# A decoder trunk on one core: a convolution tail joined on TensorE, a new order of the first blocks and of five normalizations

## The chip, the cores and the metric

The kernel runs on one core of one Trainium2 chip. A core has five engines with queues of their own: TensorE (PE; its weight loads are listed as PEld), VectorE (DVE), ScalarE (ACT), GpSimd (POOL) and SyncE (SP), which here only issues transfers. The metric is the device time of one execution in microseconds. Shown are the median of three runs and one profiled execution, from whose trace all rows come.

## The reference

One inference step of a two-layer decoder trunk, for 256 prompt tokens and 8 samples of one token, 264 columns in all, model width 2048, all in 32-bit floats. Layer 0 mixes tokens with a convolution module, layer 1 with an mLSTM; both have a gated feed-forward network and a gated addition of an embedding. The change lies in the convolution module and in the normalizations:

```python
def conformer_conv(x, past, w_in, b_in, w_dw, b_dw, ln_g, ln_b, w_out, b_out):
    a, gt = jnp.split(x @ w_in + b_in, 2, axis=-1)
    u = a * jax.nn.sigmoid(gt)
    y, new_past = causal_dwconv(u, past, w_dw, b_dw)      # 31 taps for each of 2048 channels
    y = jax.nn.silu(layer_norm(y, ln_g, ln_b))
    return y @ w_out + b_out, new_past

for i in range(DEPTH):                                    # 2 layers
    x = layer_norm(ALPHA * x + mixer(x), ln_mix_g[i], ln_mix_b[i])
    x = layer_norm(ALPHA * x + conv_ffn(x), ln_ffn_g[i], ln_ffn_b[i])
    x = x + sigmoid(x @ pl_w_gate[i]) * rms_norm(p[i] @ pl_w_proj[i], pl_g[i])
```

## The kernel before

Activations lie feature by feature: 16 chunks of 128 features (partitions) by 264 columns. A product of a weight matrix runs in blocks of output chunks. For each block the weights come from memory in raw tiles of 1 MB (512 KB where a block has one output chunk), and a half of such a tile is split: `whi` is its rounded copy (ACT, line 246), `wlo` the rest (DVE or POOL, line 247). Activations are split likewise into XH and XL, and a product is the sum of three fast ones, whi x XH, whi x XL and wlo x XH (lines 263 to 265; with LAG, lines 271, 272 and 277, the XL products one chunk later). Some halves are *native*: PE multiplies the raw 32-bit weights with X directly (line 236), for which no split is needed, and which the trace shows as two records a product.

The convolution's input product has ten blocks (`BLOCKS`). Block 0 is all native; X itself arrives during it, two chunks at a time (`load`, which `wblock` calls as a hook while it issues the weights' transfers), and is split for the later blocks. The parameter tile `par` is loaded when `load` is called with `PARK`, its second half in block 1, after which a small DVE operation on `par` follows. `NAT` says how many halves of each block are native, `VLO` how many low parts are DVE's instead of POOL's. After a block's product the gate gives U, and the 31 taps of the convolution follow for its chunk or two: `GT` taps as ACT products and POOL additions (in cscr, then joined to Y), `PT` taps on PE as products with diagonal matrices (`diags` makes these on ACT from the identity; `join_pe`), the rest on DVE. The last blocks' taps form a tail with little product work beside it.

Then comes the LayerNorm of the convolution (`ln` with silu=True). Its mean and mean square are PE products with a constant matrix (line 409): lne is a sum of two chunks of Y on DVE, lnq one of squares; between them stand `emb` products (line 516), the products p W_p of the embeddings, which are needed much later and fill PE here. The shift (a mean of the first chunks) is subtracted from chunks 12 to 15 on DVE at the end of the joins. After the reciprocal on DVE, a list of steps sets the order on DVE and ACT: `CVSEQ` here, `LNSEQ` in the four plain LayerNorms. A step is a letter, a chunk and a count: s subtracts the mean from chunks, m multiplies (and lets ACT write silu or XH), l forms XL, o copies an emb product, h marks from which half on the weights' casts come behind that point. The product with cv_w_out follows; its first four chunks are native (`WON`), with Y as operand.

`high_priority` and `after` (an order without a wait) shape the queues; within an engine, instructions run in the queue's order.

Of the kernel before, what the change touches and what calls it, by code (L numbers as in the profile page):

```python
# [12 lines left out]
F32 = mybir.dt.float32  # L13
# [26 lines left out]
GT = [4, 4, 3, 4, 4, 5, 6, 10, 9, 5]  # L40
# [5 lines left out]
VLO = {2: 3}  # L46
# [16 lines left out]
LNSEQ = ("m0:1 o0:1 m1:1 s2:2 m2:2 l0:1 o0:8 l1:1 s4:4 m4:4 l2:2 h8:0 s8:4 l4:2 m8:2 l6:1 m10:2 l7:1 l8:1 s12:4 "  # L63
         "m12:2 h14:0 l9:1 m14:2 l10:6")

CVSEQ = ("m0:1 h4:0 o0:1 m1:3 s4:4 l0:1 o0:8 l1:1 m4:4 l3:1 l2:1 s8:2 s10:1 m8:1 "
         "s11:1 l4:1 m9:1 l5:1 s13:1 s12:1 m11:1 l6:2 s14:2 m10:1 m15:1 l9:1 l8:1 m12:1 "
         "m13:2 l10:1 l11:1 l14:1 l15:1 l12:1 l13:1")
# [5 lines left out]
PARK = 8  # L74
# [4 lines left out]

XC = 4  # L80
# [10 lines left out]

BIG = 1e30
# [24 lines left out]
def _body(ctx, tc, nc, I, O):  # L117
# [52 lines left out]

    ident = const.tile([P, P], F32, name="ident")
    make_identity(nc, ident)
    ones = const.tile([P, P], F32, name="ones")
    g.memset(ones, 1.0)
# [4 lines left out]
    dummy = const.tile([P, 1], F32, name="dummy")  # L179
    mask = const.tile([P, P], F32, name="mask")  # L180
# [27 lines left out]
    wdma, wlast = [None], [None]  # L208


    def wblock(W, cols, rhs, nk, acc, k0=0, loe=None, hook=None, fine=False, native=None, hold=(), lag=0, stage=0, side=None, whole=None):
# [4 lines left out]
        for kg in range(0, nk, 2 * kq):  # L216
# [4 lines left out]
            for ka, step in ([(k, 2) for k in range(0, kn, 2)] if fine else [(0, kn)]):  # L221
# [3 lines left out]
                for c0, w in cols:  # L225
# [3 lines left out]
                    at += w  # L229
            for h0 in range(0, kn, kq):  # L230
                for f in (side or {}).get(kg + h0, ()):
                    f()
# [12 lines left out]
                with tc.high_priority(AHEAD):  # L245
                    whi = s.copy(hi[:, :, :width], r)  # L246
                    wlo = e.tensor_tensor(lo[:, :, :width], r, f32(hi[:, :, :width]), ALU.subtract)  # L247
                for k, first in hold:
# [110 lines left out]
    def ln(Y, gn, bn, off, outs, silu=False, acc=None, emb=(), pq=None, behind=None, steps=LNSEQ):  # L359
# [83 lines left out]
        if silu:  # L443
            sub(2, 2)
        dv(v.reciprocal(r, r))
        for op, c, n in _seq(steps):
# [10 lines left out]
    ln_state = None  # L457

# [84 lines left out]
    def conv_mixer():  # L543
# [16 lines left out]
        def diags():  # L560
# [12 lines left out]
        def load(k, n):  # L573
            dma.dma_start(X[:, k:k + n], I["xT"][:, k:k + n])
            if k == PARK:
                dma.dma_start(par[:, :NPC], I["par"][:, :NPC])
            for c in range(k, k + n):
                split(XH[:, c], XL[:, c], X[:, c])
# [3 lines left out]
        joins, tails, late, later, tapped, formed = [], [], [], [], [None], [None]  # L582
        for bi, (c0, n) in enumerate(blocks):
# [32 lines left out]
            with tc.high_priority(2 * AHEAD if last else GLU):  # L616
# [4 lines left out]
                for j in range(n):  # L621
# [4 lines left out]
                    s.copy(w, u)  # L626
# [591 lines left out]
```

## Time and profile before

| what | value |
|---|---|
| time, median of 3 runs | 2523.67 us (2522.7 to 2524.24) |
| profiled execution | 2524.14 us, span 2522.4 us |
| PE busy | 2504.5 us (99%) |
| DVE, ACT, POOL busy | 1613.7 (64%), 1256.9 (50%), 235.0 us (9%) |

The span is the time from the first to the last record of the profile; the execution's own time has some 1.7 us around it. The granted clock of TensorE is given as a share of full speed. In the timeline a row is a run of like instructions on one engine: its start, its length, what it is and how many, and in brackets the idle time ahead of it and what ended that.

### The profile page before, as it was taken

What the parts mean: (1) busy time and instruction counts of PE and PEld (TensorE: products, weight loads), DVE (VectorE), ACT (ScalarE), POOL (GpSimd) and SP (SyncE); (2) the same over time, 40 slices, a digit from 0 to 9 for tenths busy, and PEclk for the clock granted to TensorE, in tenths of its full rate; (3) what the DMA queues carried; (4) which work ended last, traced back from release to release, by engine and by line L of the source; (5) the groups of instructions that cost most, each with busy time, mean ns of one, the idle gap of its engine ahead of it and who ended that gap; (6) DMA issues with size and microseconds to landing.
All of it is one profiled execution on the core that took longest, in us unless ns stands there. A gap on an engine that the chain in (4) does not pass through costs nothing.

```text
span 2522.4 us, 47218 instructions
## 1 busy us (share of the span) xinstructions
PE 2504.5 (99%) x20000; PEld 2478.1 (98%) x20000; DVE 1613.7 (64%) x2429; ACT 1256.9 (50%) x1773; POOL 235.0 (9%) x203
## 2 busy tenths in 40 slices
PE   9999999999999999999999999999999999999999
PEld 8998999999999999999999999999999999999999
DVE  6898586555445555488678787775555445555586
ACT  6556464444334444346566666464444334444363
POOL 6985000000000000000010011000000000000000
PEclk9999999999999999999999999999999999999999
DMA  7646546555555556545687786555555555656553
GB/s 254 192 152 215 184 147 201 184 183 177 177 183 184 184 178 206 181 163 193 202 293 243 235 285 220 197 180 184 181 177 180 183 184 169 190 178 206 184 172 135
DMA packets 271110, 486.54 MB, mean 193 GB/s; under 512 B 12170, under 2 KB 72330, under 8 KB 270482
## 3 DMA queue, kind: packets, MB, share of 16 engines
q1 hardware_dynamic: 263410, 456.19, 55.9%
q0 software_dynamic: 7488, 27.33, 3.1%
q8 instruction: 156, 2.56, 0.4%
q14 instruction: 56, 0.46, 0.1%
HBM read 465.77 MB, written 19.68 MB: 192 GB/s over the span
## 4 chain that ended last, share of the span: by engine, by line
PE 89%; DVE 6%; issue 2%; DMA 1%; POOL 1%; ACT 1%; SPq 0%; POOLq 0%; DVEq 0%
PE acc L264 27%; PE acc L263 27%; PE acc L265 27%; PE acc L236 2%; DVE Y L149 2%; DVE X L149 1%; PE acc L277 1%; DVE X L146 1%; DVE wlo L247 1%; POOL cscr L146 1%; PE acc L271 1%; DVE XL L149 1%; PE acc L272 1%; DMA spare<-scr 0%; DMA raw<-in_cv_w_in 0%
## 5 line engine op out<-in xcount | busy, mean ns | idle before, releaser
L247 DVE TENSOR_TENSOR wlo<-raw,whi 128x1024 fp32r<-128x1024 f32 x749 | 916.9, 1227 | 731.4 <-ACT whi L246 730.0
L246 ACT CAST whi<-raw 128x1024 fp32r<-128x1024 f32 x794 | 828.8, 1048 | 1022.1 <-PE acc L264 965.4
L264 PE MATMUL acc<-XL,whi 128*128 128x264 f32 x3840 | 1088.1, 284 | 0.0
L263 PE MATMUL acc<-XH,whi 128*128 128x264 f32 x3840 | 1084.1, 285 | 0.4 <-ACT whi L246 0.3
L265 PE MATMUL acc<-XH,wlo 128*128 128x264 f32 x3840 | 1083.8, 284 | 0.4 <-POOL wlo L247 0.3
L264 PEld LDWEIGHTS acc<-XL,whi 128*128 128x128 f32 x3840 | 722.7, 188 | 0.5
L263 PEld LDWEIGHTS acc<-XH,whi 128*128 128x128 f32 x3840 | 720.5, 189 | 1.5 <-ACT whi L246 0.5
L265 PEld LDWEIGHTS acc<-XH,wlo 128*128 128x128 f32 x3840 | 719.0, 188 | 1.2 <-POOL wlo L247 1.0
L264 PE MATMUL acc<-ha,whi 128*128 128x264 f32 x1024 | 290.5, 284 | 0.0
L265 PE MATMUL acc<-ha,wlo 128*128 128x264 f32 x1024 | 290.3, 284 | 0.0
L263 PE MATMUL acc<-ha,whi 128*128 128x264 f32 x1024 | 288.8, 285 | 0.0
L247 POOL TENSOR_TENSOR wlo<-raw,whi 128x1024 fp32r<-128x1024 f32 x45 | 109.4, 2444 | 1724.8 <-ACT whi L246 1724.8
L263 PE MATMUL acc<-xo,whi 128*128 128x264 f32 x768 | 223.6, 291 | 0.0
L264 PE MATMUL acc<-xo,whi 128*128 128x264 f32 x768 | 220.6, 287 | 0.0
L265 PE MATMUL acc<-xo,wlo 128*128 128x264 f32 x768 | 219.9, 286 | 0.0
L264 PEld LDWEIGHTS acc<-ha,whi 128*128 128x128 f32 x1024 | 192.8, 188 | 0.1
L265 PEld LDWEIGHTS acc<-ha,wlo 128*128 128x128 f32 x1024 | 192.3, 188 | 0.0
L263 PEld LDWEIGHTS acc<-ha,whi 128*128 128x128 f32 x1024 | 192.0, 189 | 0.1
L263 PEld LDWEIGHTS acc<-xo,whi 128*128 128x128 f32 x768 | 144.8, 189 | 0.7
L264 PEld LDWEIGHTS acc<-xo,whi 128*128 128x128 f32 x768 | 144.7, 188 | 0.8
L265 PEld LDWEIGHTS acc<-xo,wlo 128*128 128x128 f32 x768 | 144.5, 188 | 0.3
L149 DVE SCALAR_TENSOR_TENSOR Y<-U,par,Y 128x227 f32<-128x227 f32 (+24 forms) x337 | 131.7, 452 | 13.1 <-ACT Y L627 8.2
(294 smaller groups left out, 2578.9 us busy)
## 6 DMA issues: line engine op xcount, KB each, us to landing
raw<-in_ff_w_gate SPq DMA_DIRECT2D x88, 1024.0 KB, 5.2
raw<-in_ff_w_up SPq DMA_DIRECT2D x88, 1024.0 KB, 5.1
raw<-in_ff_w_down SPq DMA_DIRECT2D x88, 1024.0 KB, 5.0
raw<-in_pl_w_gate SPq DMA_DIRECT2D x32, 1024.0 KB, 5.2
raw<-in_ml_w_in SPq DMA_DIRECT2D x32, 1024.0 KB, 6.6
raw<-in_cv_w_in SPq DMA_DIRECT2D x60, 512.0 KB, 5.9
raw<-in_cv_w_out SPq DMA_DIRECT2D x16, 1024.0 KB, 5.0
raw<-in_ml_w_in SPq DMA_DIRECT2D x32, 512.0 KB, 4.7
```

The lines of the kernel that those rows point to most:

```text
L146: return e.tensor_tensor(o, a, b, op)
L149: return v.scalar_tensor_tensor(o, a, sc, b, op0, op1)
L236: pe.matmul(acc[j], raw[:, kc - kg, j * P:(j + 1) * P], (whole or X)[:, kc], start=kc == 0, stop=kc == nk - 1)
L246: whi = s.copy(hi[:, :, :width], r)
L247: wlo = e.tensor_tensor(lo[:, :, :width], r, f32(hi[:, :, :width]), ALU.subtract)
L263: pe.matmul(acc[j], wh, xh, start=kc == 0, stop=False)
L264: pe.matmul(acc[j], wh, xl, start=False, stop=False)
L265: wlast[0] = pe.matmul(acc[j], wl, xh, start=False, stop=kc == nk - 1)
L271: pe.matmul(acc[j], hi[:, k2, j * P:(j + 1) * P], xh, start=kc == 0, stop=False)
L272: wlast[0] = pe.matmul(acc[j], lo[:, k2, j * P:(j + 1) * P], xh, start=False, stop=False)
L277: pe.matmul(acc[j], whs[j], xl, start=False, stop=k0_ == nk - 1)
```

## The change

- Six products of a matrix of ones (128 columns, `WARM`) go to PE ahead of all else; ones is made first on POOL.
- Block 0: the first two chunks of weights and of X are loaded one by one, X's on ACT's queue; `par` follows with chunk 12 instead of 8.
- Block 1: `VLO` gives all three low parts to DVE.
- The diagonal matrices are ordered behind a later copy.
- Chunk 15 has seven ACT and POOL taps instead of five; `join_pe` starts each sum with a product of the negative identity and the shift and covers all columns, and the four DVE subtractions of the shift go.
- `CVSEQ` is rewritten: nothing is subtracted from chunks 2 and 3 ahead of the reciprocal, steps cover up to four chunks, and XH of the chunks is POOL's, that of the native four in one operation (step c).
- `LNSEQ`, used by all four plain LayerNorms, is changed in three places.
- The first POOL operations of the first feed-forward network are ordered behind POOL's casts of XH.

```diff
-GT = [4, 4, 3, 4, 4, 5, 6, 10, 9, 5]
+GT = [4, 4, 3, 4, 4, 5, 6, 10, 9, 7]
-VLO = {2: 3}
+VLO = {1: 8, 2: 3}
-LNSEQ = ("m0:1 o0:1 m1:1 s2:2 m2:2 l0:1 o0:8 l1:1 s4:4 m4:4 l2:2 h8:0 s8:4 l4:2 m8:2 l6:1 m10:2 l7:1 l8:1 s12:4 "
-         "m12:2 h14:0 l9:1 m14:2 l10:6")
+LNSEQ = ("m0:1 o0:1 m1:1 s2:2 m2:2 l0:1 o0:8 l1:1 s4:4 m4:1 l2:1 m5:1 l3:1 m6:2 h8:0 s8:4 l4:2 m8:2 l6:1 m10:2 "
+         "l7:1 l8:2 s12:4 m12:2 h14:0 l10:1 m14:2 l11:5")
+CVSEQ = ("m0:1 o0:1 m1:1 s2:2 m2:2 h4:0 o0:8 s4:4 m4:4 h8:0 s8:4 l4:2 m8:4 l6:2 c0:4 s12:4 m12:4 h12:0 "
+         "l8:2 l10:2 l0:4 l12:2 l14:2")
-PARK = 8
+PARK = 12
-XC = 4
+WARM = 6
...
+    ones = const.tile([P, P], F32, name="ones")
+    g.memset(ones, 1.0)
+    idle = psM.tile([P, 512], F32, name="idle", tag="mi")
+    for _ in range(WARM):
+        pe.matmul(idle[:, :P], ones, ones, start=True, stop=True)
...
+    nident = const.tile([P, P], F32, name="nident")
+    s.mul(nident, ident, -1.0)
...
+                    step = 1 if kg + ka < 2 else 2
+                    fetch(ka, step)
...
-                    ac(s.copy(outs[0][:, k], Y[:, k])) if k < XC else g.tensor_copy(outs[0][:, k], Y[:, k])
+                    if k // 2 not in WON:
+                        pooled.append(g.tensor_copy(outs[0][:, k], Y[:, k]))
...
-        if silu:
-            sub(2, 2)
         dv(v.reciprocal(r, r))
...
+            if op == "c":
+                after(g.tensor_copy(outs[0][:, c:c + n], Y[:, c:c + n]), ac.last)
+                continue
...
-                act(d, ident, AF.Copy, scale=pc("cv_w_dw", c * CW + t))
+                after(act(d, ident, AF.Copy, scale=pc("cv_w_dw", c * CW + t)), copied[0])
...
-            dma.dma_start(X[:, k:k + n], I["xT"][:, k:k + n])
+            with tc.high_priority(3 * AHEAD if k < 2 else 0):
+                (s if k < 2 else dma).dma_start(X[:, k:k + n], I["xT"][:, k:k + n])
...
                     acc = accs(1)[0]
+                    pe.matmul(acc, nident, shift, start=True, stop=False)
                     for t in range(t0, t0 - pt, -1):
                         tapped[0] = pe.matmul(acc[:, 30 - t:SEQ], diag[c0 + j, t], U4[j][:, 0:226 + t],
-                                              start=t == t0, stop=t == t0 - pt + 1)
-                    o = Y[:, c0 + j, 30 - t0:SEQ]
-                    tt(o, acc[:, 30 - t0:SEQ], o, ALU.add)
+                                              start=False, stop=t == t0 - pt + 1)
+                    o = Y[:, c0 + j]
+                    tt(o, acc, o, ALU.add)
...
-                for k in range(12, 16):
-                    tt(Y[:, k], Y[:, k], shift, ALU.subtract)
...
+        for ins in first if i == 0 else ():
+            after(ins, pooled[-1])
```

The order of instructions on three engines shows what moves. First DVE's queue around the end of block 0 and in block 1, before (U and us are the gate's outputs, `Y<-U,par,Y` is one tap, xs the samples' taps):

```order
L149 SCALAR_TENSOR_TENSOR U<-acc_113,par,cscr 128x256
L149 SCALAR_TENSOR_TENSOR us<-acc_113,par,cscr 128x8
L149 SCALAR_TENSOR_TENSOR par<-par 128x32
L149 SCALAR_TENSOR_TENSOR Y<-U,par,Y 128x250
L149 SCALAR_TENSOR_TENSOR Y<-U,par,Y 128x249
L149 SCALAR_TENSOR_TENSOR Y<-U,par,Y 128x248
L149 SCALAR_TENSOR_TENSOR Y<-U,par,Y 128x247
```

The same stretch of DVE's queue in the changed kernel:

```order
L148 SCALAR_TENSOR_TENSOR U<-acc_122,par,cscr 128x256
L148 SCALAR_TENSOR_TENSOR us<-acc_122,par,cscr 128x8
L261 TENSOR_TENSOR wlo<-raw,whi 128x1024
L148 SCALAR_TENSOR_TENSOR Y<-U,par,Y 128x250
L148 SCALAR_TENSOR_TENSOR Y<-U,par,Y 128x249
L148 SCALAR_TENSOR_TENSOR Y<-U,par,Y 128x248
L148 SCALAR_TENSOR_TENSOR par<-par 128x32
L148 SCALAR_TENSOR_TENSOR Y<-U,par,Y 128x247
L148 SCALAR_TENSOR_TENSOR Y<-U,par,Y 128x246
L148 SCALAR_TENSOR_TENSOR Y<-U,par,Y 128x245
L261 TENSOR_TENSOR wlo<-raw,whi 128x1024
L148 SCALAR_TENSOR_TENSOR Y<-U,par,Y 128x244
```

Two low parts of block 1 now stand among its taps, the first of them ahead of all taps and the second behind six taps and the operation on par.

Second, ACT's queue in the tail, after the square root of the convolution's LayerNorm (line 519, now 537, copies emb products; line 424, now 439, is the silu; line 425 made XH), before:

```order
L439 ACTIVATE acc_2459<-acc_2459,epst 128x264
L519 COPY u_109<-acc_2484 128x264
L519 COPY u_109<-acc_2487 128x264
L424 ACT_TABLE_LOAD
L424 ACTIVATE Y<-Y,par 128x264
L425 CAST XH<-Y 128x264
L519 COPY u_109<-acc_2490 128x264
L246 CAST whi<-raw 128x1024 x3
L424 ACTIVATE Y<-Y,par 128x264
L246 CAST whi<-raw 128x1024
L425 CAST XH<-Y 128x264
```

The same stretch of ACT's queue in the changed kernel:

```order
L455 ACTIVATE acc_2473<-acc_2473,epst 128x264
L537 COPY u_118<-acc_2498 128x264
L537 COPY u_118<-acc_2501 128x264
L439 ACT_TABLE_LOAD
L439 ACTIVATE Y<-Y,par 128x264
L537 COPY u_118<-acc_2504 128x264
L439 ACTIVATE Y<-Y,par 128x264 x3
L537 COPY u_118<-acc_2507 128x264
L537 COPY u_118<-acc_2510 128x264
L260 CAST whi<-raw 128x1024 x2
L439 ACTIVATE Y<-Y,par 128x264 x4
```

The silus of chunks 1 to 3 now directly follow the first, the weights' casts come behind them, and the XH casts are gone from ACT.

Third, DVE's queue in the first plain LayerNorm, behind the subtraction of chunks 4 to 7 (`X<-X,par,lnq` is step m, `XL<-X,par,XH` step l, `X<-X,lnm` step s), before:

```order
L149 SCALAR_TENSOR_TENSOR X<-X,par,lnq 128x264 x4
L149 SCALAR_TENSOR_TENSOR XL<-X,par,XH 128x264 x2
L146 TENSOR_TENSOR X<-X,lnm 128x1056
L149 SCALAR_TENSOR_TENSOR XL<-X,par,XH 128x264 x2
L247 TENSOR_TENSOR wlo<-raw,whi 128x1024
L149 SCALAR_TENSOR_TENSOR X<-X,par,lnq 128x264 x2
L149 SCALAR_TENSOR_TENSOR XL<-X,par,XH 128x264
L149 SCALAR_TENSOR_TENSOR X<-X,par,lnq 128x264 x2
L149 SCALAR_TENSOR_TENSOR XL<-X,par,XH 128x264
L247 TENSOR_TENSOR wlo<-raw,whi 128x1024 x2
L149 SCALAR_TENSOR_TENSOR XL<-X,par,XH 128x264
L146 TENSOR_TENSOR X<-X,lnm 128x1056
```

The same stretch of DVE's queue in the changed kernel:

```order
L148 SCALAR_TENSOR_TENSOR X<-X,par,lnq 128x264
L148 SCALAR_TENSOR_TENSOR XL<-X,par,XH 128x264
L148 SCALAR_TENSOR_TENSOR X<-X,par,lnq 128x264
L148 SCALAR_TENSOR_TENSOR XL<-X,par,XH 128x264
L148 SCALAR_TENSOR_TENSOR X<-X,par,lnq 128x264 x2
L145 TENSOR_TENSOR X<-X,lnm 128x1056
L148 SCALAR_TENSOR_TENSOR XL<-X,par,XH 128x264 x2
L148 SCALAR_TENSOR_TENSOR X<-X,par,lnq 128x264 x2
L148 SCALAR_TENSOR_TENSOR XL<-X,par,XH 128x264
L148 SCALAR_TENSOR_TENSOR X<-X,par,lnq 128x264 x2
L148 SCALAR_TENSOR_TENSOR XL<-X,par,XH 128x264
L261 TENSOR_TENSOR wlo<-raw,whi 128x1024 x3
```

The first XL of this stretch (chunk 2) now follows one multiplication instead of four, and three low parts of weights stand together. The next rows of the changed kernel are the XL of chunks 8 and 9 and then the subtraction of the last four chunks, which stood between those two before.

## Rows read from the trace of the kernel before

**Rows 1.** The page: engines over the span, and VectorE's costliest group.
```profile
PE 2504.5 (99%) x20000; PEld 2478.1 (98%) x20000; DVE 1613.7 (64%) x2429; ACT 1256.9 (50%) x1773; POOL 235.0 (9%) x203
...
L247 DVE TENSOR_TENSOR wlo<-raw,whi 128x1024 fp32r<-128x1024 f32 x749 | 916.9, 1227 | 731.4 <-ACT whi L246 730.0
```

**Rows 2.** PE by windows: stretch in us, busy (records), granted clock, DMA share, GB/s.
```profile
4.00:9.30 5.30, 5.26 (x12) 1.00 1.02 319
9.30:20.80 11.50, 11.50 (x52) 1.00 1.08 344
```

**Rows 3.** Timeline of PE, ACT, DVE and POOL, 0 to 40: start, us, engine, operation.
```profile
31.76 0.39 PE L263 MATMUL acc<-XH,whi 128*128 128x264 f32 x1 [0.32 <-ACT whi L246]
...
35.60 0.39 PE L265 MATMUL acc<-XH,wlo 128*128 128x264 f32 x1 [0.18 <-POOL wlo L247]
...
11.72 4.78 ACT L569 ACTIVATE u<-ident,par 128x128 f32<-128x128 f32 x16
...
20.91 1.04 ACT L246 CAST whi<-raw 128x1024 fp32r<-128x1024 f32 x1 [2.54 <-DMA raw<-in_cv_w_in]
...
25.15 0.19 DVE L149 SCALAR_TENSOR_TENSOR par<-par 128x32 f32<-128x32 f32 x1 [0.75 <-DMA par<-in_par]
27.39 3.03 DVE L149 SCALAR_TENSOR_TENSOR Y<-U,par,Y 128x250 f32<-128x250 f32 x6 [2.05 <-ACT Y L627]
...
34.46 2.17 DVE L247 TENSOR_TENSOR wlo<-raw,whi 128x1024 fp32r<-128x1024 f32 x1 [1.08 <-ACT whi L246]
...
30.09 2.41 POOL L247 TENSOR_TENSOR wlo<-raw,whi 128x1024 fp32r<-128x1024 f32 x1
```

**Rows 4.** All engines by windows: busy (x) of PE, PEld, DVE, ACT, POOL, clock, DMA.
```profile
10.00:20.00 10.00, 10.00 (x47) 8.54 (x46) 3.52 (x10) 7.46 (x25) 0.00 (x0) 1.00 1.09 345
```

**Rows 5.** Timeline of PE, 224 to 242.
```profile
227.11 0.71 PE L409 MATMUL lnm<-lne,onesD 128*128 128x264 f32 x2 [1.04 <-DVE lne L146]
...
233.42 1.60 PE L236 MATMUL acc<-Y,raw 128*128 128x264 f32 x6 [0.26 <-ACT Y L424]
237.49 4.85 PE L236 MATMUL acc<-Y,raw 128*128 128x264 f32 x13 [2.46 <-ACT Y L424]
```

**Rows 6.** Timeline of ACT, DVE and POOL, 228 to 245.
```profile
232.76 0.61 ACT L424 ACTIVATE Y<-Y,par 128x264 f32<-128x264 f32 x1 [0.56 <-DVE Y L146]
...
233.99 2.94 ACT L246 CAST whi<-raw 128x1024 fp32r<-128x1024 f32 x3
236.83 0.61 ACT L424 ACTIVATE Y<-Y,par 128x264 f32<-128x264 f32 x1
...
230.46 1.81 DVE L445 RECIPROCAL acc<-acc 128x264 f32<-128x264 f32 x1
...
241.92 2.22 POOL L425 CAST XH<-Y 128x264 fp32r<-128x264 f32 x4 [18.94 <-ACT Y L424]
```

**Rows 7.** All engines in one window of the tail, columns as in rows 4.
```profile
237.40:241.60 4.20, 4.11 (x11) 3.22 (x12) 4.20 (x7) 4.04 (x10) 0.00 (x0) 0.61 0.68 222
```

**Rows 8.** First plain LayerNorm, PE and DVE; then waits: us in total, times, longest.
```profile
345.54 0.75 PE L277 MATMUL acc<-XL,whi 128*128 128x264 f32 x4 [0.25 <-DVE XL L149]
...
356.63 0.75 PE L277 MATMUL acc<-XL,whi 128*128 128x264 f32 x4 [0.59 <-DVE XL L149]
...
345.00 0.89 DVE L149 SCALAR_TENSOR_TENSOR XL<-X,par,XH 128x264 fp32r<-128x264 f32 x2
...
356.09 0.49 DVE L149 SCALAR_TENSOR_TENSOR XL<-X,par,XH 128x264 fp32r<-128x264 f32 x1
...
PE acc L277 <- DVE XL L149: 3.5, 8, 0.6
```

**Rows 9.** Join products of L683 (min/median/max ns); DVE and POOL before the tail.
```profile
L683 PE MATMUL acc<-u,u x32: 364/368/370, 208.8 to 215.2; 128*128 128x244 f32 x6, 128*128 128x243 f32 x6, 128*128 128x242 f32 x6, 128*128 128x241 f32 x6
...
218.42 0.61 DVE L146 TENSOR_TENSOR Y<-Y,lnshift 128x264 f32<-128x264 f32 x1
...
219.57 0.80 POOL L146 TENSOR_TENSOR sf<-sf,par 128x352 f32<-128x352 f32 x1
```

More of the change, by code (lines that the diff above doesn't have):

```diff
@@ L206, in split @@
         return s.copy(hi, src), tt(lo, src, f32(hi), ALU.subtract)
-    wdma, wlast = [None], [None]
+    wdma, wlast, wsplit = [None], [None], [None, None]
     def wblock(W, cols, rhs, nk, acc, k0=0, loe=None, hook=None, fine=False, native=None, hold=(), lag=0, stage=0, side=None, whole=None):
@@ L220, in wblock, with fetch @@
                 raw = raw.rearrange("p a (b m) -> p (a b) m", b=2)
-            for ka, step in ([(k, 2) for k in range(0, kn, 2)] if fine else [(0, kn)]):
+            def fetch(ka, step):
                 if hook:
@@ L229, in wblock @@
                     at += w
+            if not fine:
+                fetch(0, kn)
             for h0 in range(0, kn, kq):
+                ka = h0
+                while fine and ka < h0 + kq:
+                    step = 1 if kg + ka < 2 else 2
+                    fetch(ka, step)
+                    ka += step
                 for f in (side or {}).get(kg + h0, ()):
@@ L247, in wblock @@
                     wlo = e.tensor_tensor(lo[:, :, :width], r, f32(hi[:, :, :width]), ALU.subtract)
+                wsplit[:] = whi, wlo
                 for k, first in hold:
@@ L457, in _body @@
     ln_state = None
+    pooled = []
     def residual(name, off, first=None):
@@ L577, in load @@
             for c in range(k, k + n):
-                split(XH[:, c], XL[:, c], X[:, c])
+                for ins, w in zip(split(XH[:, c], XL[:, c], X[:, c]), wsplit):
+                    if w:
+                        after(ins, w)
         blocks = BLOCKS
         nb = len(blocks)
-        joins, tails, late, later, tapped, formed = [], [], [], [], [None], [None]
+        joins, tails, late, later, tapped, formed, copied = [], [], [], [], [None], [None], [None]
         for bi, (c0, n) in enumerate(blocks):
@@ L625, in conv_mixer @@
                     stt(us[:, ch], a[:, SEQ:], pc("cv_b_in", ch), sg[:, j, SEQ:], ALU.add, ALU.mult)
-                    s.copy(w, u)
+                    copied[0] = s.copy(w, u)
                     act(Y[:, ch, :SEQ], w, AF.Identity, bias=pc("cv_b_dw", ch), scale=pc("cv_w_dw", ch * CW + 30))
@@ L1051, in ffn @@
         fo = smp.tile([P, NF, 18], F32, name="fo", tag="fo")
-        g.tensor_copy(fo[:, :, 0:8], sf[:, :, 1])
+        first = [g.tensor_copy(fo[:, :, 0:8], sf[:, :, 1])]
         w = pc("ff_w_dw", i * 3 * NF, 3 * NF).rearrange("p (r c) -> p r c", r=3)
         for r in range(2):
-            tt(sf[:, :, r], sf[:, :, r], w[:, r].unsqueeze(2).to_broadcast([P, NF, NB]), ALU.mult, e=g)
+            first.append(tt(sf[:, :, r], sf[:, :, r], w[:, r].unsqueeze(2).to_broadcast([P, NF, NB]), ALU.mult, e=g))
+        for ins in first if i == 0 else ():
+            after(ins, pooled[-1])
         tt(sf[:, :, 0], sf[:, :, 0], sf[:, :, 1], ALU.add, e=g)
```

5 lines of the change are left out of this document (removed).

## The prediction, made before the result was known

> **What bounds the kernel now.** I read the page first. TensorE (PE) is busy for 2504.5 us, 99% of the span [rows 1], so the reader is to see that only the few places where PE waits or runs slowly can pay. I then listed PE's records by start time; where one starts later than its predecessor's pitch (0.121 us a split product, 0.222 us a record of an unsplit product, which is two records), the excess is lost time. It sums to about 38 us over the program, and three stretches that the change touches hold most of what it can reach.
>
> *The start.* PE's first product starts at 4.0; the first twelve records take 0.44 each, the next 52 take 0.22 [rows 2]: the first stretch runs at the pace of 1.2 GHz, though the column of the granted clock reads 1.00 there. Slow pace costs 12 x 0.22 = 2.6 us. Block 0's 64 records end at 20.8, and ScalarE's first cast of block 1's weights starts at 20.91 after waiting 2.54 for their DMA [rows 2, 3]. So PE and the transfers arrive together, and in the 10 us before that the transfers ran without a break, at 345 GB/s [rows 4]. After that, PE loses time at four places in blocks 1 and 2. The largest, at 31.76, is idle for 0.32 by the profile and 0.49 late from start to start, behind a cast; the others, at 28.16, 35.60 and 38.95, come 0.20, 0.34 and 0.32 late behind GpSimd's low parts; 1.35 in all [rows 3].
>
> *The tail of the convolution.* PE waits for VectorE's last chunk sum until 227.11 (1.31 from start to start), for the first silu until 233.42 (0.43), and for the second until 237.49 (2.62) [rows 5]. The cause of the last stands on ScalarE: the silu of chunk 1 at 236.83 is queued behind three weight casts that began at 233.99 [rows 6]. Right after this wait the clock is granted at 0.61 on average, of which PE's records show 1.2 GHz: 11 records in 4.11 us, where 18 fit at 0.222, so 7 x 0.22 = 1.5 us [rows 7]. Together 5.9.
>
> *The four plain LayerNorms.* In each, PE waits twice for XL: at 345.54 (0.42 from start to start) for chunk 2, which VectorE forms only at 345.00 behind four multiplications, and at 356.63 (0.76) for chunk 9, formed at 356.09 behind a subtraction of four chunks and two multiplications [rows 8]. The view of waits counts eight of each, two a LayerNorm [rows 8]: 4 x 1.2 = 4.7 us.
>
> **The change, part by part.**
>
> *Idle products and single chunks.* Six 128-column products of ones precede the first real one, so some of the twelve slow records would be fast, and the first chunk, half as large, can start earlier. Bytes to be moved before block 1's weights are the same, so 20.91 stays (four single transfers instead of two cost issue time on SP, which I bound at 0 to +0.3). Whatever PE wins before, it waits for at 20.9: 0. The cover is the transfer; if that ended sooner, up to 2.6 would come out.
>
> *Block 1's low parts on VectorE, one split at a time.* GpSimd's low part takes 2.41, VectorE's 1.15 to 2.17 (2.17 is the one at 34.46, while GpSimd was working; elsewhere on the page the mean is 1.23) [rows 1, 3]. Three of them, 7.2 us, leave GpSimd, whose queue had set the waits at 28.16, 35.60 and 38.95. But the new order puts the second one behind six taps (3.03 a six, [rows 3]) and behind the small operation on par that waits for a transfer until 25.15 [rows 3]. It starts near 26.85 and ends 28.0 to 29.0, where PE wants it at 27.85: a new wait of 0.2 to 1.15. Behind it VectorE's taps of block 1 queue; nobody waits for these before their join, some blocks later. Up to 1.35 saved less 0.2 to 1.15: I take -0.5 (range +0.5 to -1.5), the middle, since the third weight block also is issued sooner, when GpSimd is free. The Trainium skill (GPSIMD Engine Reference, section "1. Specifications") says that GpSimd shares its SBUF interfaces with VectorE and that two-input instructions contend; the 2.17 beside 1.23 agrees, and by it the wait would be at its long end, +0.9 on this term.
>
> *Diagonal matrices.* Two batches of 16 ScalarE operations (4.78 for the one at 11.72, [rows 3]; the other, at 42.2, takes the same) move to block 3. The order deals them out there in groups of one to six between casts and taps, and ScalarE is busy half of the span [rows 1]: 0. If a cast for PE came behind a group of six, it would be 6 x 0.3 = 1.8 late, and the splits are made ahead by more than that; I keep +0.5 as the upper bound, inside the start's range.
>
> *Join.* Four native products with the negative identity replace four VectorE subtractions: +4 x 0.444 = +1.78 on PE, whose other join products keep 0.37 each [rows 9]. VectorE drops two taps of chunk 15 (0.5 each by the 3.03 for six, [rows 3]; here, shorter, 0.45) and four subtractions (0.61, [rows 9]), so its last chunk sum is ready near 225.0 instead of 227.05, while PE now comes for it at 227.5: the wait of 1.31 becomes none. GpSimd gets two more additions for these taps (0.7 to 0.9 each) but loses three sf and fo operations that stand among them (0.80 for the one at 219.57, [rows 9]; 2.4 together), so its chain ends as before; if the additions took 0.9 and the three had been hidden, it would end 1.8 later, still ahead of the last chunk sum.
>
> *Silu order.* ScalarE now issues silus 0 to 3 back to back and casts weights behind them; VectorE multiplies two chunks at once and goes straight to the reciprocal (1.81 us [rows 6]) with no third subtraction ahead of it. Before, the reciprocal began at 230.46, behind three subtractions, and the silu at 232.76 [rows 6]. Now PE's last sum of squares ends 0.45 later (1.78 less the wait of 1.31), and the reciprocal, behind two subtractions, begins at 230.3; with 1.81, 0.44 for the multiplication and 0.6 for the silu, chunk 0 is done at 233.25, and PE, through its emb products 0.45 later than before, is free at 233.45. Silu 1 follows at 234.1 (due 234.8), 2 at 234.9 (236.1), 3 at 235.4 (237.4). Each of 32 native records then takes 0.222, no wait, and no fall of the clock: all of 0.43 + 2.62 + 1.53 goes. Behind them the first three weight casts come later, their low parts end at 239.1, and XH of chunks 4 on is GpSimd's (0.55 a chunk, [rows 6]): XL 6 and 7 at 245.1 (due 245.4), XL 8 and 9 at 248.2 (248.3), a low part at 251.85 (251.8). Nothing is spare there, and I charge 0.2. Sum of the tail: -5.9 + 1.8 + 0.2 = -3.9 (range -2, where the five near ties just named cost another 0.4 each, to -4.1, where none does).
>
> *LayerNorm lists.* Chunk 2's XL follows one multiplication, not four: ready at 344.28, due 345.12. Chunk 9's follows chunk 8's, ahead of that subtraction. Three low parts now stand together ahead of chunk 8's XL, which ends at 354.1, up to 0.3 late, and chunk 14's XH comes behind three casts on ScalarE, some 0.24 late. Of 1.2 remain 0.54: -0.65 each, -2.6 for four (range -1, where the two late ones cost 0.2 more each, to -4.7, where neither is late).
>
> **Sum.** -0.5 - 3.9 - 2.6 = -7.0. Against the profiled execution's 2524.14 us (span 2522.4 and 1.7 around it) 2517.1; the median of the runs lies 0.47 below that execution, so 2516.8 (0.2% of the time, about what a measurement of this kernel can tell from no change, is 5.05 us: 2518.6 and 2528.7 are its ends).
>
> **The rivals.**
>
> *The start pays too.* If early products bring the clock up and the transfers have slack that the profile hides, the whole 2.6 comes out: 2514.2. Against it stands the 2.54 us for which ScalarE waits for the weights at 20.91 [rows 3]. The Trainium skill (TensorE: Matmul & The Clock Gate, section "Why this matters for your kernels") tells to warm TensorE up with products before its work counts; rows here show the slow first twelve records, and not yet the remedy.
>
> *VectorE and ScalarE bound the tail.* VectorE is busy throughout 237.4 to 241.6 [rows 7], so PE's earlier arrival may find the splits not ready: half of the 3.9 or more comes back, 2518.6 to 2521.5.
>
> *The lists only move the waits.* As many XL come late at chunks 8 and 14 as were late at 2 and 9: the 2.6 falls away, 2519.4.
>
> *Slower: GpSimd's casts.* It now makes XH for all sixteen chunks, one operation of four chunks among the single ones; VectorE's XL queue behind these in order, and behind them low parts for PE. Each late us is one of PE, and a wait like that at 237.49 costs its clock besides: 2.46 + 1.53 = 4 [rows 5, 7]. Two such waits, 8, outweigh 7.0: 2525. Decides from 7.0 us of lateness on. GpSimd's pace of 0.55 a chunk speaks against it.
>
> **How the numbers follow.** Forecast (2514.5 to 2518.6) 0.50; start pays 0.12; tail bound 0.25, of which 0.10 still under 2518.6; lists 0.08; slower 0.05, of which 0.03 over 2528.7. Faster by over 0.2%: 0.50 + 0.12 + 0.10 = 0.72; within 0.2%: 0.15 + 0.08 + 0.02 = 0.25; slower 0.03. The range from 2512.8 (the start pays and the lists leave no wait) to 2521.5 leaves out the slower case and the ends of the others.
>
> **What would show it.** Right: block 0's twelve slow records fewer or gone, and PE idle before 20.9 for the weights; a short wait for DVE's low part near 28; PE's native products without a gap from about 233, clock 1.00 throughout; one or two waits of under 0.4 in each LayerNorm. Wrong: the cast of block 1's weights starting well before 20.9, or PE waiting for XL or low parts between 240 and 255.

## The result, and the profile after

The changed kernel's median is 2526.3 us (2521.08 to 2534.15, 22 runs) beside 2523.28 us (2521.5 to 2527.82, 22 runs) for the kernel before: ratio 1.0013 [1.0007, 1.0019]. That lies inside the 0.2% within which the prediction counts no change, on its slow side; the forecast was 2516.8 and a range that ends at 2521.5. The profiled execution took 2526.93 us, with a span of 2525.2, against 2524.14 and 2522.4.

The page of the kernel after, engines over the span (before: [rows 1]):

```profile
PE 2508.8 (99%) x20020; PEld 2483.1 (98%) x20020; DVE 1612.3 (64%) x2410; ACT 1255.7 (50%) x1772; POOL 237.0 (9%) x203
```

What PE waited for in the kernel before, over the whole program (total us, times, longest us):

```profile
PE acc L236 <- DMA raw<-in_cv_w_in: 4.0, 1, 4.0
...
PE acc L236 <- ACT Y L424: 2.7, 2, 2.5
PE lnm L409 <- DVE lne L146: 1.0, 1, 1.0
PE hq L939 <- DVE hq L146: 0.8, 1, 0.8
...
```

The lines left out are the XL wait of [rows 8], 3.5 in eight, and 0.6 at the places of [rows 3]. The same view of the kernel after:

```profile
PE acc L280 <- DVE wlo L261: 4.0, 3, 2.9
PE hq L959 <- DVE hq L145: 2.5, 1, 2.5
PE acc L278 <- ACT psg L1128: 1.6, 2, 0.8
PE idle L175 <- POOL ones L171: 1.0, 1, 1.0
PE acc L278 <- DVE fo L1095: 0.6, 2, 0.3
PE acc L250 <- DMA raw<-in_cv_w_in: 0.5, 1, 0.5
PE acc L292 <- DVE XL L145: 0.5, 1, 0.5
```

Every wait that the change aimed at is gone: the silus (2.7), lne (1.0) and the eight XL (3.5). Others stand there that were not: one of 2.9 and two of 0.5 for VectorE's low parts, two for psg, two for fo, and one of 2.5 where 0.8 was, on a product (hq) that the change does not touch.

To see where time is won and lost, the start of the same PE product can be compared in both traces, by counting records from the program's start (the added products set aside). After minus before, in us:

| place (start in the trace before) | offset after |
|---|---|
| first product, 4.0 | -0.33 |
| record 12 of block 0 | -1.56 |
| last record of block 0 | -0.54 |
| block 1, 34 | +3.33 |
| ahead of the tail, 148 | +2.74 |
| behind the joins, 224 (with 1.78 of added products) | +4.35 |
| behind the tail, 267 | -0.93 |
| first plain LayerNorm, 363, and behind it, 382 | -1.91, -0.67 |
| second, 1137 and 1152 | -1.70, -0.65 |
| mLSTM, 1485 | +2.55 |
| third, 1660 and 1674 | +1.50, +2.75 |
| fourth, 2444 and 2462 | +1.71, +2.80 |

So the start cost 2.74 where it was to win 0.5; the tail won 3.67 (forecast 3.9); the four LayerNorms together lost 0.5 where they were to win 2.6 (each wins about 1.0 and loses 1.0 to 1.3 right behind); and the mLSTM between them lost 3.2. One execution is not the kernel: two more traces of the changed kernel stand at +1.69 ahead of the tail, and two more of the kernel before at -0.93 and -0.50, so the start's loss is 1.7 at the least and 3.7 at the most.

**The start.** Timeline of PE in the kernel after, block 0 and the middle of block 1:

```profile
16.93 5.36 PE L250 MATMUL acc<-X,raw 128*128 128x264 f32 x23 [0.54 <-DMA raw<-in_cv_w_in]
...
27.43 0.28 PE L279 MATMUL acc<-XL,whi 128*128 128x264 f32 x1
30.65 0.59 PE L280 MATMUL acc<-XH,wlo 128*128 128x264 f32 x1 [2.94 <-DVE wlo L261]
31.03 0.42 PE L278 MATMUL acc<-XH,whi 128*128 128x264 f32 x1
```

DVE and POOL in the same stretch:

```profile
26.15 0.19 DVE L148 SCALAR_TENSOR_TENSOR par<-par 128x32 f32<-128x32 f32 x1 [0.70 <-DMA par<-in_par]
26.26 1.49 DVE L148 SCALAR_TENSOR_TENSOR Y<-U,par,Y 128x247 f32<-128x247 f32 x3
27.66 2.93 DVE L261 TENSOR_TENSOR wlo<-raw,whi 128x1024 fp32r<-128x1024 f32 x1
...
27.47 2.04 POOL L145 TENSOR_TENSOR xs<-xs,par 128x960 f32<-128x960 f32 x1 [0.41 <-DMA xs<-in_sconv]
29.47 1.70 POOL L145 TENSOR_TENSOR cscr<-cscr 128x251 f32<-128x251 f32 x1
```

PE wants block 1's second low part at 27.55. VectorE begins it at 27.66, behind the operation on par, for whose transfer it stood idle for 0.70, and three taps. It takes 2.93 for it beside two GpSimd operations, where the first low part, at 22.81 with GpSimd idle, took 1.23. PE waits 3.10 from start to start, and then runs split products at a pitch of 0.22 (1.2 GHz) until 33.9. The granted clock shows it, in PE, PEld, DVE, ACT, POOL by windows, the clock in the column after these:

```profile
30.00:40.00 10.00, 9.35 (x64) 9.35 (x65) 8.05 (x15) 5.39 (x9) 7.50 (x4) 0.83 0.71 235
```

In the kernel before it reads 1.00 there. About 13 records at 0.22 instead of 0.121 are 1.3 us more.

**The tail.** PE in the kernel after (before: [rows 5]):

```profile
230.25 0.61 PE L424 MATMUL lnm<-lne,onesD 128*128 128x264 f32 x2
...
236.03 7.29 PE L250 MATMUL acc<-Y,raw 128*128 128x264 f32 x32
...
248.70 0.76 PE L292 MATMUL acc<-XL,whi 128*128 128x264 f32 x4 [0.54 <-DVE XL L145]
```

The last lne product and the 32 native records follow without a gap, at 0.222 each; the window of [rows 7] now shows a clock of 1.00. One of the near ties, XL of chunk 8, is late by 0.69 from start to start, where 0.2 was charged in all; a wait for XL between 240 and 255 was one of the prediction's signs of being wrong. All twelve traces with the whole of the tail's edit gain 3.6 to 3.7 from 148 to behind the tail.

**The LayerNorms.** PE in and behind the first, and behind the second:

```profile
368.86 0.39 PE L280 MATMUL acc<-XH,wlo 128*128 128x264 f32 x1 [0.50 <-DVE wlo L261]
370.42 0.36 PE L278 MATMUL acc<-XH,whi 128*128 128x264 f32 x1 [0.32 <-DVE fo L1095]
...
1147.06 0.39 PE L278 MATMUL acc<-XH,whi 128*128 128x264 f32 x1 [0.76 <-ACT psg L1128]
```

Both XL waits are gone, and of chunk 8's XL 0.31 is left (at 353.25, from start to start), as charged. So PE comes about 1.0 earlier to the next products, and waits there. ACT ahead of these two places:

```profile
364.88 1.74 ACT L480 ACTIVATE X<-X,par 128x264 f32<-128x264 f32 x4
366.51 1.04 ACT L260 CAST whi<-raw 128x1024 fp32r<-128x1024 f32 x1
...
1145.32 1.28 ACT L1128 ACT_TABLE_LOAD   x1
1146.61 0.96 ACT L1128 ACTIVATE psg<-acc 128x264 f32<-128x264 f32 x3
```

Behind the first, the weights' cast stands behind residual operations (line 480), and the low part behind the cast. Behind the second, the sigmoid starts at 1146.61, which in the kernel before was 1146.87, though PE was 1.7 earlier at 1137: ScalarE, with its casts and the table load, sets the time.

### The profile page after: what moved, and what is told of

Its sections match the earlier page's. It is cut to its first block, busy times and chain, and to the rows that moved or that the text cites. A ratio compares the mean times of both kernels' runs of the same rounds, so it can differ in the third digit from the quotient of the medians.

```text
span 2525.2 us, 47254 instructions
## 1 busy us (share of the span) xinstructions
PE 2508.8 (99%) x20020; PEld 2483.1 (98%) x20020; DVE 1612.3 (64%) x2410; ACT 1255.7 (50%) x1772; POOL 237.0 (9%) x203
## 4 chain that ended last, share of the span: by engine, by line
PE 90%; DVE 4%; ACT 2%; issue 2%; DMA 2%; SPq 0%; POOL 0%; ACTq 0%; DVEq 0%; POOLq 0%
PE acc L279 28%; PE acc L278 28%; PE acc L280 28%; PE acc L250 2%; DVE X L148 1%; DVE wlo L261 1%; ACT whi L260 1%; DVE X L145 1%; DVE XL L148 1%; DMA spare<-scr 1%; PE acc L705 1%; ACT X L480 0%; DMA par<-in_par 0%; SPq L232 0%; DMA X<-in_cT 0%
## 5 line engine op out<-in xcount | busy, mean ns | idle before, releaser
L261 POOL TENSOR_TENSOR wlo<-raw,whi 128x1024 fp32r<-128x1024 f32 x42 | 101.5, 2432 | 1705.0 <-ACT whi L260 1700.5
L148 DVE SCALAR_TENSOR_TENSOR Y<-U,par,Y 128x238 f32<-128x238 f32 (+24 forms) x337 | 131.2, 455 | 11.7 <-ACT Y L648 8.5
```

The lines of the kernel that those rows point to most:

```text
L148: return v.scalar_tensor_tensor(o, a, sc, b, op0, op1)
```

## The experiments

The theory after the result: the order of the queues in block 1 (casts and low parts behind taps) makes the wait at 27.55. That order is chosen when the kernel is built, by the scheduler that fills the queues, and it takes the single chunks and the idle products together for it to come out so. The rivals: VectorE's low parts as such; the single chunks' transfers or the idle products as such; the new `LNSEQ`; and chance, from one execution to the next. "At 148" and "behind the tail" below are offsets of PE to the trace before, as in the table.

**The changed kernel once more** (no edit), and again later:

> The changed kernel itself, unchanged, for a second profile. Theory A (the loss is made in block 1: PE waits for the second low part on VectorE and then runs at 1.2 GHz): PE again waits 2 to 3.5 us for a VectorE low part near 27 to 31 and is 2 to 3.5 us behind the kernel before when the convolution's tail begins; time 2525 to 2528. Theory B (the loss is the wait for the scratch transfer in the mLSTM near 1478, in code that the change does not touch): that wait is again 1.7 us longer than before's 0.97, if it is the change's; if it is chance, it comes out near 1 and the time falls by 3.

> The changed kernel once more: the wait near 27 is 3 us and the slow products follow it, whenever the weights land; the wait in the mLSTM lies between 0.5 and 3.

2524.54 us (2522.15 to 2534.59, 10 runs), ratio 1.0007 [0.9998, 1.0017], just below the time expected; the later single run 2522.91. PE is 1.69 behind at 148 in both. It waits 3.13 and 2.98 at the same place, with weights that came 1.2 to 1.7 earlier (first cast at 20.08 and 20.49 instead of 21.73), and the window from 30 to 40 reads a clock of 0.83 in both. The wait belongs to this kernel, not to one execution. The low part began at 26.78 and 27.19 and took 2.85 and 2.26, again beside GpSimd. The mLSTM wait was 2.34 and 0.60 instead of 2.69.

**Block 1's low parts back on GpSimd.**

```diff
-VLO = {1: 8, 2: 3}
+VLO = {2: 3}
```

> Block 1's low parts back on GpSimd, all else as in the changed kernel. Theory A: the wait of 3.1 near 27.4 and the slow products behind it go, three waits of 0.2 to 0.5 like those of before come back; PE is 1 us ahead or level at the tail's start instead of 2.7 behind; time 2522 to 2523, 3 to 4 below the changed kernel. Theory B: no change at the end, 2526.

2524.95 us (10 runs), ratio 1.0004 [0.9994, 1.0014], where 2522 to 2523 was expected; +1.73 at 148, as in the last two traces. The wait does not go, it divides: PE waits four times for GpSimd, 3.5 in all. POOL there, and PE's longest:

```profile
24.65 2.37 POOL L145 TENSOR_TENSOR cscr<-cscr 128x254 f32<-128x254 f32 x3
26.97 2.37 POOL L261 TENSOR_TENSOR wlo<-raw,whi 128x1024 fp32r<-128x1024 f32 x1
...
29.39 0.39 PE L280 MATMUL acc<-XH,wlo 128*128 128x264 f32 x1 [1.46 <-POOL wlo L261]
```

On GpSimd too the second low part stands behind taps. So VectorE as such is not the cause.

**The kernel before with only this part.**

```diff
-VLO = {2: 3}
+VLO = {1: 8, 2: 3}
```

> The kernel before with block 1's low parts on VectorE and nothing else. Here two low parts stand ahead of all of VectorE's taps of block 1. Theory A in its narrow form (the place behind six taps costs, not VectorE as such): no wait over 0.5 for a low part near 28, and 0 to 1.3 us faster than before, 2522 to 2523.5. Wide form (VectorE is the wrong engine there): 1 to 4 us slower than before.

2528.43 us (10 runs), ratio 1.0019 [1.001, 1.0029], slower than either form expected. The low parts alone win 1.72 by 41, but later PE waits 2.00 at 108 and 2.04 at 215.9, and 0.5 longer for lne. ScalarE at the first place:

```profile
107.81 1.99 ACT L246 CAST whi<-raw 128x1024 fp32r<-128x1024 f32 x2 [7.46 <-DMA raw<-in_cv_w_in]
```

A cast sat 7.46 us on a late transfer, and the operations that free PE's accumulators queued behind it. Why the transfer came late here is not shown. "Nobody waits for these before their join" holds in the changed kernel, whose PE has no wait between block 1 and the tail.

**Old `LNSEQ`.**

```diff
-LNSEQ = ("m0:1 o0:1 m1:1 s2:2 m2:2 l0:1 o0:8 l1:1 s4:4 m4:1 l2:1 m5:1 l3:1 m6:2 h8:0 s8:4 l4:2 m8:2 l6:1 m10:2 "
-         "l7:1 l8:2 s12:4 m12:2 h14:0 l10:1 m14:2 l11:5")
+LNSEQ = ("m0:1 o0:1 m1:1 s2:2 m2:2 l0:1 o0:8 l1:1 s4:4 m4:4 l2:2 h8:0 s8:4 l4:2 m8:2 l6:1 m10:2 l7:1 l8:1 s12:4 "
+         "m12:2 h14:0 l9:1 m14:2 l10:6")
```

> The old list of steps for the four plain LayerNorms, all else as changed. Theory C (the new list takes away 1.2 us of waits in each LayerNorm, and PE waits for the same time for weight splits or free accumulators some 15 us later): time within 1 us of the changed kernel, the two waits of 0.4 and 0.8 back in each LayerNorm, and the waits of 0.5 to 1.1 behind it (near 368, 1146, 1674, 2452) gone. Rival (the lists gain what was forecast and something else loses it): 2 to 3 us slower than the changed kernel.

2524.4 us (10 runs), ratio 1.0004 [0.9995, 1.0014]. Its waits of PE:

```profile
PE acc L292 <- DVE XL L148: 3.5, 8, 0.6
PE acc L280 <- DVE wlo L261: 2.8, 1, 2.8
```

The 3.5 are back, and of the lines of the kernel after, psg (1.6), fo (0.6) and 1.2 of the low parts' 4.0 are gone: 3.5 for 3.4. The new list exchanges one set of waits for another.

**First two chunks loaded together; no idle products.** Two kernels, each with one of the edits:

```diff
-                    step = 1 if kg + ka < 2 else 2
+                    step = 2
...
-            with tc.high_priority(3 * AHEAD if k < 2 else 0):
-                (s if k < 2 else dma).dma_start(X[:, k:k + n], I["xT"][:, k:k + n])
+            dma.dma_start(X[:, k:k + n], I["xT"][:, k:k + n])
```

> The changed kernel with the first two chunks loaded together again, X's on SP's queue; idle products, low parts on VectorE, tail and lists stay. In this kernel ScalarE casts block 1's second half ahead of the taps and VectorE makes its low parts ahead of all its taps. Theory A2 (the start loses because its transfers come 0.8 to 1.6 us later and because the splits of block 1 then stand behind taps): weights land at 20.8 and 23.9 again, the wait of 3 near 27 is under 0.5, PE is 0 to 2 us ahead of the kernel before at the tail's start instead of 1.7 behind; time 3 to 4 us below the changed kernel, about 2521. Rival (the wait near 27 only moves on, since VectorE's taps are now later, as when the low parts alone were moved): PE loses it again between 100 and 225, 2524.

```diff
-WARM = 6
+WARM = 0
```

> The changed kernel without the six idle products; the single chunks stay. The splits of block 1 stand ahead of the taps here too. It tells the transfers from the order: if the order made the wait, it is gone here although the transfers are as late as in the changed kernel (21.7 and 25.5), and PE is level or 1 us ahead of before in block 2; if late transfers made it, a wait of 1.5 to 3 near 27 stays. Of the idle products themselves I expect nothing: the twelve slow records are back and block 0 still ends with the weights' landing.

2523.09 us, ratio 0.9997 [0.9988, 1.0006], and 2522.11 us, ratio 0.9994 [0.9984, 1.0003] (10 runs each); +0.34 and -1.54 at 148. In both, casts and low parts stand ahead of the taps again and the long wait is gone (0.67 with the chunks together, none without the idle products). With the chunks together the time is still 2 above what was expected: PE loses 1.05 again between 60 and 120. Without idle products PE runs block 0 with no gap:

```profile
3.31 20.37 PE L250 MATMUL acc<-X,raw 128*128 128x264 f32 x80 [3.31 <-DMA X<-in_xT]
```

So the idle products win nothing at block 1, as forecast, and removing either edit takes the wait away. Whether that comes from the order or from the edits themselves, the order forced by hand must tell:

**The order alone.** The changed kernel, with ScalarE's taps of block 0 ordered behind block 1's last cast and VectorE's behind its last low part, all else kept:

```diff
+        held = [], []
...
+                for e in range(2):
+                    for ins in held[e]:
+                        after(ins, wsplit[e])
...
+                    if bi == 0:
+                        held[0].extend(early)
...
+                        if c0 == 0:
+                            held[1].append(ins)
```

> The changed kernel, idle products, single chunks and all, with one thing added: an order (no wait) that puts block 0's ScalarE taps behind block 1's last weight cast and block 0's VectorE taps behind its last low part, as the queues stand where one of the two start edits is left out. If the order alone made the loss in the start: the wait of 3.1 near 27 is under 0.5, the slow products behind it are gone, PE is 0 to 2 us ahead of the kernel before near 148 instead of 1.5 to 2.7 behind, time 3 to 4.5 below the changed kernel, 2520 to 2523. If the idle products or the single chunks cost by themselves: less than half of that.

2522.09 us (2520.08 to 2527.73, 11 runs), ratio 0.9996 [0.9987, 1.0005]. VectorE, GpSimd and PE at the place:

```profile
26.12 0.19 DVE L148 SCALAR_TENSOR_TENSOR par<-par 128x32 f32<-128x32 f32 x1 [2.62 <-DMA par<-in_par]
26.56 1.22 DVE L261 TENSOR_TENSOR wlo<-raw,whi 128x1024 fp32r<-128x1024 f32 x1 [0.25 <-ACT whi L260]
27.71 3.10 DVE L261 TENSOR_TENSOR wlo<-raw,whi 128x1024 fp32r<-128x1024 f32 x1
...
27.38 2.34 POOL L145 TENSOR_TENSOR xs<-xs,par 128x960 f32<-128x960 f32 x1 [25.41 <-DMA raw<-in_cv_w_in]
...
27.84 0.39 PE L280 MATMUL acc<-XH,wlo 128*128 128x264 f32 x1 [0.51 <-DVE wlo L261]
```

The low part that PE wants begins at 26.56, ahead of GpSimd's sum, and takes 1.22; the next, which begins 0.33 into that sum, takes 3.10 and holds PE up by only 0.23. The wait is 0.67 from start to start, the clock reads 1.00 from 30 to 40, and the offset at 148 is -0.49. In the four later kernels with this order it is +0.21, -0.93, -0.74 and -2.03. The order is the cause of the start's loss: it sets when the low part begins, and what GpSimd is doing by then. That the start then wins anything is not shown, since the kernel before itself varies by 0.9.

**The tail alone.** The start, `VLO`, `LNSEQ`, `PARK` and the diagonals are as before; of the edit the three constants:

```diff
-VLO = {1: 8, 2: 3}
+VLO = {2: 3}
...
-PARK = 12
+PARK = 8
...
-WARM = 6
+WARM = 0
```

> The kernel before with the tail's part of the change alone (seven taps, the negative identity, the new list after the reciprocal, GpSimd's casts); start, low parts, diagonal matrices and the four plain LayerNorms as before. If the tail's sum was right (-3.9 forecast, -3.7 read from the trace): 2519.3 to 2520.5. If the tail needs the rest of the change (GpSimd freed, diagonals moved): 2522 to 2524.

From 148 to behind the tail its PE gains 3.58, and in the whole profiled execution (2519.62 us) 4.50. Yet the median of 10 runs is 2523.33, ratio 0.9998 [0.9988, 1.0007]: five runs lie at 2519.4 to 2521.9 and five at 2524.7 to 2527.5. The gain of the tail is in the trace; the median does not show it. Which waits the slower five had, no trace shows.

**Chunks together and old `LNSEQ`** (the edits of the two kernels above, in one):

> As e5, with the old list for the four plain LayerNorms as well. If the lists are worth nothing in sum: the same as e5 within 1 us. If the wait in the mLSTM near 1478 is longer with the new lists (2.69, 2.34 and 1.74 in the three profiles with them, 0.97, 0.75 and 0.53 in the three without) and is made by them: 1 to 2 us below e5.

2521.93 us (10 runs), ratio 0.9994 [0.9984, 1.0003]; -0.96 at 148, -4.68 behind the tail, -3.60 at the end. Its wait in the mLSTM is 1.93 with the old list, so the new one does not make that wait; 1.16 below the kernel with the chunks together is within the spread.

**The residual operations moved.** The order's kernel, with the 16 of line 480 behind the first casts of the up product:

```diff
-        residual("ff_b_down", i * NC, hold[2].last)
...
+                if cb == 0:
+                    residual("ff_b_down", i * NC, wsplit[0])
```

> As e9, and in the two feed-forward networks ScalarE's 16 residual operations stand behind the weight casts of the first up block instead of ahead of the last casts of the first gate block. If the LayerNorm lists' gain was lost to these 16 operations (casts come late, PE waits 0.67 and 0.48 some 15 us after the LayerNorm): both waits go in the first and the third LayerNorm, 2 x 1.15 = 2.3 us below e9. If PE's waits there are bound by something else (VectorE's release of accumulators): 0.

2519.67 us (11 runs), ratio 0.9986 [0.9978, 0.9995]. The waits behind the first and third LayerNorms are gone, and PE keeps 1.29 and 1.16 there. Those behind the second and fourth (psg) stay, at 0.74 and 0.83. In two of the four LayerNorms the list's gain thus stays once ScalarE's queue is free; for the other two no run shows it.

**The order with the old `LNSEQ`:**

> As e9, with the old lists for the four plain LayerNorms. If the lists are worth 0 in sum: within 1 us of e9. If they are worth the forecast 2.6: 2.6 above e9.

2522.8 us (11 runs), ratio 0.9998 [0.9989, 1.0007], beside 2522.09 with the new one: the same, as with the first exchange of lists.

**The shift subtracted on VectorE again,** in the order's kernel:

```diff
-                    pe.matmul(acc, nident, shift, start=True, stop=False)
...
-                                              start=False, stop=t == t0 - pt + 1)
-                    o = Y[:, c0 + j]
-                    tt(o, acc, o, ALU.add)
+                                              start=t == t0, stop=t == t0 - pt + 1)
+                    o = Y[:, c0 + j, 30 - t0:SEQ]
+                    tt(o, acc[:, 30 - t0:SEQ], o, ALU.add)
...
+                for k in range(12, 16):
+                    tt(Y[:, k], Y[:, k], shift, ALU.subtract)
```

> As e9, with the four VectorE subtractions of the shift back in place of PE's four products with the negative identity (seven taps of chunk 15 stay off PE and VectorE). PE saves 1.78 and comes for the last chunk sum near 225.7 on before's clock; VectorE has 4 x 0.6 more to do and is ready near 227.4. If the exchange was even: within 0.7 us of e9, with a wait of 1.5 to 1.9 for the last chunk sum back in the tail. If VectorE had slack: 1.8 below e9.

2519.62 us (11 runs), ratio 0.9983 [0.9974, 0.9992]. From 148 to behind the tail it gains 5.48, the order's kernel 3.70: the difference is the 1.78 of the four products, and no wait takes their place. DVE's last lne and PE's product of it:

```profile
223.41 0.43 DVE L145 TENSOR_TENSOR lne<-Y 128x264 f32<-128x264 f32 x1 [0.81 <-PE acc L424]
...
224.99 0.61 PE L424 MATMUL lnm<-lne,onesD 128*128 128x264 f32 x2
```

VectorE waits for PE here, not PE for VectorE. The rest of the change (two taps fewer on VectorE among it) had ended the wait already; the negative identity paid 1.78 for nothing.

**The kernel before, two more looks:**

> The kernel before, unchanged, for another profile. If the wait in the mLSTM near 1479 is chance: it lies anywhere from 0.5 to 3 and the time from issue to use of the scratch transfer from 6.7 to 9.1 us, as in the profiles of the other kernels. If it belongs to the changed kernels: it is 0.5 to 1.2 again.

> The kernel before once more, for a third profile: the wait in the mLSTM 0.5 to 3 if it is chance, 0.5 to 1.2 if it belongs to the changed kernels.

2527.31 and 2524.23 us. In the first, DVE and PE in the mLSTM:

```profile
1476.86 0.17 DVE L146 TENSOR_TENSOR nf<-sn,spare 128x8 f32<-128x8 f32 x1 [5.54 <-DMA spare<-scr]
...
1481.74 0.76 PE L939 MATMUL hq<-hq,onesD 128*128 128x264 f32 x2 [2.71 <-DVE hq L146]
```

The kernel before has this wait too, at 2.87, 0.97 and 0.99 from start to start in its three traces. It follows the transfer through scratch memory (`spare<-scr`), which from its issue to its use on DVE took 9.51, 7.46 and 7.77 us; in the kernel after and its repeats 9.06 (wait 2.69), 8.40 (2.34) and 7.34 (0.60). One and the same kernel meets a short wait and a long one, so the length is chance, and both kernels meet it. Whether the long one is more frequent in the changed kernel, three traces of each cannot tell.

**The three repairs together** (the order, the residual operations and the shift on VectorE; the edits above):

> The changed kernel with all three repairs: block 1's splits ahead of block 0's taps, the residual operations behind the first up block's casts, the four subtractions back on VectorE. If the three terms are the whole of the error: e12 less 2.4, or 2517 to 2518, PE 8 us ahead of the kernel before at the end apart from what the mLSTM wait takes. If they overlap (PE, coming 1.8 earlier to the LayerNorms, waits there for something else): 2518.5 to 2519.5.

2517.7 us (2515.55 to 2524.8, 11 runs) beside 2523.79 for the kernel before: ratio 0.9979 [0.997, 0.9988]. It beats the kernel before; the changed kernel's interval lies wholly above this one. Its page, and its waits of PE:

```profile
PE 2503.2 (100%) x20012; PEld 2478.8 (99%) x20012; DVE 1613.7 (64%) x2414; ACT 1257.4 (50%) x1772; POOL 237.6 (9%) x203
...
PE hq L970 <- DVE hq L145: 2.5, 1, 2.5
PE acc L278 <- ACT psg L1140: 1.6, 2, 0.8
PE idle L175 <- POOL ones L171: 1.0, 1, 1.0
PE acc L280 <- POOL wlo L261: 0.7, 1, 0.7
```

This execution caught a long mLSTM wait (2.5) and still has a span of 2515.4, 7.0 under that of the kernel before; the time is the one expected of it, and PE is 8.7 ahead until the mLSTM. That -7.0 is also the forecast for the change is luck: the sum is another one (-2.0 at the start, -5.5 in the tail, -2.4 in the LayerNorms, +3.0 in the mLSTM), and the kernel has two edits that were not in the change and lacks one that was.

## Why the prediction was wrong, step by step

**Idle products and single chunks: right in size, wrong in being harmless.** By record 12 PE was 1.56 ahead, by the end of block 0 only 0.54, after waiting for weights at 16.93; a kernel without idle products reaches block 1 no later. What I missed: together the two edits, costed at nothing, moved the scheduled order of other work, which is the next point.

**Block 1's low parts: the step that failed.** I forecast a new wait of 0.2 to 1.15 and put the term at -0.5. I had the place and the reason (behind six taps and par), and mis-sized it: 3.10, which is 1.95 over its long end. Of that 0.81 is the later start of the low part (27.66 for 26.85; the operation on par stood at 26.15 instead of 25.15), 0.76 its length (2.93 for the 2.17 that I took as its longest), 0.3 that PE came earlier. The 2.17 was no upper bound: that low part began when GpSimd's operation had 1.09 left, this one when 1.85 were left, and both ended 1.08 behind it. The clock behind the wait, 1.3 us, was not in the sum at all, though [rows 7] had shown the same after 237.49. Term: +2.74 instead of -0.5 (+1.69 in two more traces). With the order put right it measured -0.49 in one trace, and +0.21 to -2.03 in four more, about level with the kernel before (0 to -0.93). The Trainium skill (GPSIMD Engine Reference, section "1. Specifications") says that VectorE and GpSimd share SBUF interfaces and contend where VectorE reads two inputs. The row with 2.93 beside GpSimd's work agrees, and exceeds the one that I had taken as the upper bound.

**Diagonal matrices: no wait of PE names them;** right as far as the trace shows.

**Join and silu order: right.** -3.67 measured in the changed kernel, -3.58 with the tail alone, against -3.9; the clock stayed at 1.00 as forecast. The XL of chunk 8 cost 0.69 where 0.2 was charged in all. But the term of +1.78 for the negative identity, correct as a cost, bought nothing: I credited it with the end of the 1.31 wait, and without it that wait is gone too.

**LayerNorm lists: failed; a rival came true in its size, by another mechanism.** "The lists only move the waits" had 0.08, by lateness at chunks 8 and 14. Within the LayerNorms the lists won about 1.0 each, more than the 0.65 of the sum, with 0.31 late at chunk 8. The waits moved further on: 12 to 25 us later, to the low part behind the residual operations and to the sigmoid. There each LayerNorm returns 1.0 to 1.3. The step left out was the question who is late next when PE comes 1 us earlier; ScalarE was on no list of mine there.

**The other rivals.** Early products did not pay; VectorE and ScalarE bound the tail by no more than the 0.69; GpSimd's casts made no wait of the size that was to turn the sign.

**mLSTM: not in the prediction.** The 3.2 there are the longer wait (2.69 for 0.97) and, behind it, some 14 products at a pitch of 0.22 (1.4): chance in a scratch transfer, without which the trace after would end near the trace before. By part, -0.5 - 3.9 - 2.6 = -7.0 became +2.7 - 3.7 + 0.5 = -0.5. The 22 runs' median nevertheless lies 3.0 above that of the kernel before, and the repeat's 0.5 above its own. Why stays open: no trace shows those runs, and a long mLSTM wait in more of them is a rival that was not tested.

**Slips in the sums,** of no consequence here: 2517.1 less 0.47 is 2516.6, not 2516.8; the low part's wait at its long end makes that term -0.2, which is 0.3 and not 0.9 above the -0.5; and the start's 2.6 and lists without a wait put the lower end of the range at 2512.1, not 2512.8.

## What to carry to other kernels

Where a scheduler makes the queues' order, an edit that costs nothing by itself can still be dear by what it reorders: compare the order around the next wait, and hold it with an explicit order where a low part or cast is due. Before counting a removed wait as won, follow the waiting engine to its next two or three operands and ask when those would be ready; here 3.5 us of waits came back as 3.4. Price a low part on VectorE by what GpSimd has begun before it, and a wait with the slow stretch that can stand behind it.

## What the runs showed of the hardware

- A low part on VectorE (128x1024) took 1.23 us alone, and 1.22 where it began ahead of GpSimd's sum xs (26.56 and 27.38, with the order put right). Where xs had begun first, it ended 1.08 to 1.09 us after xs, whenever it had itself begun: it took 2.93, 2.85 and 2.26 us in three traces of the changed kernel, and 3.10 for the second one with the order put right.
- After PE's wait of 3.10 the granted clock read 0.83 from 30 to 40 and split products came at a pitch of 0.22; in three more executions with that order the same window read 0.83 too. Not each such wait is followed by this: behind the mLSTM wait of 2.69 in the kernel after the clock read 0.78 from 1478 to 1484, behind one of 2.98 (without idle products) it read 1.00. The Trainium skill (TensorE: Matmul & The Clock Gate, section "Why this matters for your kernels") warns of gaps between TensorE's products as a cause of a lower clock; the traces with the waits of 3.10 and 2.69 agree, the one with 2.98 shows no fall.
- One and the same transfer through scratch memory took between 6.7 and 9.5 us from issue to use in different executions. In one execution of the kernel before, PE was 0.23 ahead of another just before the wait for it (2.87 for 0.97) and, after the slow products behind the wait, 3.18 behind.
